# Scan of a hybrid backbone: copies out of PSUM on one engine, and two buffers for the queries

## Chip, cores and metric

The kernel runs on one core of a Trainium2 chip. The metric is the time of one execution on the device in microseconds (us). Engines are named as in the profile: PE is TensorE, PEld its weight loads, DVE is VectorE, ACT is ScalarE, POOL is GpSimd, SP is SyncE, which issues most of the DMAs.

## The reference

Two layers of a backbone over 512 latent tokens and 256 context tokens, 1024 wide: the first mixes tokens by attention, the second by a state that is updated token by token (RWKV-7), once in each direction. Each mixer is followed by a SwiGLU block. The change lies in the second mixer, whose core is

```python
def _wkv_scan(S0, decay, k, v, kk, a, r, reverse):
    ...
    def step(S, inp):
        w_t, k_t, v_t, kk_t, a_t = inp[:5]
        sa = jnp.einsum('bhvk,bhk->bhv', S, -kk_t)
        S = (S * w_t[:, :, None, :] + sa[..., None] * (kk_t * a_t)[:, :, None, :]
             + v_t[..., None] * k_t[:, :, None, :])
        y = jnp.einsum('bhvk,bhk->bhv', S, inp[5]) if len(inp) == 6 else None
        return S, y
    S, ys = lax.scan(step, S0, tuple(jnp.moveaxis(z, 1, 0) for z in xs), reverse=reverse)
```

for 16 heads of 64 channels. The context's tokens have no queries `r` and give no `y`; their last state starts the scan of the latents. After it come a group norm, a gate, an output projection and the second SwiGLU block.

## The kernel before

The scan is done in blocks of 64 tokens: inside a block by matrix products, from block to block by a state of 64 x 64 per head. The tokens are cut into three parts p of 256 tokens: p = 0 is the context, p = 1 and 2 are the latents, taken from the front for direction d = 0 and from the back for d = 1. The 16 heads are two groups g of 8 heads, each held in four tiles f. A stage is a pair (p, g); there are six (line 1351).

Three functions make up a stage:

- `elem(p, f)` (lines 1063 to 1142) makes a tile's elementwise quantities: decays, keys, and for p > 0 the queries. It loads `kt` (keys) and `rt` (queries) from DRAM with `load` (line 1034 for p > 0, a DMA issued by SyncE). VectorE makes `R`, the decayed queries (line 1107), and overwrites `rt` with the product with the keys (line 1109); TensorE reads that once more for the bonus `bp` (line 1114), and only then is `rt` free. For p = 0 nothing is loaded into `rt`; it is scratch memory there (lines 1098 and 1099). `rt` has one buffer (`bufs=1`). `elem` also sends matrices out for the scan (lines 1096, 1097, 1104, 1108) and fills `AB`, the triangular blocks that are to be inverted.
- `invert(st)` (lines 1145 to 1203) inverts the blocks of one group by substitution, as a long row of short VectorE instructions (lines 1158, 1163, 1167, 1169) between block transposes (1149, 1172, 1173), and then merges 32 x 32 blocks by small matmuls (1184, 1198, 1200) into `Xs`.
- `scan(p, g)` (lines 1235 to 1317) goes through four steps i. A step decays the state to `S` (line 1251), copies it into `Tt` (1252, 1253), transposes a block of keys (1262, 1263), for p > 0 forms `GR` (1273, 1274), and then runs this chain:

```python
pp = ...                                              # 1281: 32 matmuls
nc.scalar.copy(Pb[HS[0], :, :, 0], pp[HS[0]])         # 1282
nc.vector.tensor_copy(Pb[HS[1], :, :, 1], pp[HS[1]])  # 1283
pu = ...                                              # 1287: 16 matmuls, with Xs
nc.scalar.copy(Tt[HS[0], 0], pu[HS[0]])               # 1289
nc.vector.tensor_copy(Tt[HS[0], 1], pu[HS[1]])        # 1290
pn = ...                                              # 1296: 32 matmuls, then Sn = pn + S (1301)
```

`HS[0]` and `HS[1]` are the lower and the upper 64 partitions. `pp` and `pu` are PSUM tiles of 128 x 512 fp32, each copied out in two halves of 64 x 512: one by ScalarE, one by VectorE. `Sn` is the next step's state. For p > 0 the step's output `py` (lines 1310, 1311) is copied (1316) and sent to DRAM.

Lines 1351 to 1360 set the program's order: scan of a stage, inversion of the next, `elem` of the one after. It is not the order on the engines. The kernel is built with a scheduler that simulates a timeline (line 1494) and places the instructions of `scan`, `invert`, `elem` and, at the end, `readout` between one another on each engine; an engine then runs its own queue in order. A tile pool adds waits where a buffer is used again. Before the first stage with queries, `project_r` (line 1320) computes the queries into DRAM; the pool `sB` (line 1344) is laid over the memory that it used. The tile `R` and the step's `GR`, `Rb` and `y` lie in `sB`. Behind the scan, `readout` (line 1386) loads the outputs of both directions and applies norm and gate; then come the output projection and the SwiGLU block.

Of the kernel before, what the change touches and what calls it, by code (L numbers as in the profile page):

```python
# [10 lines left out]
F32 = mybir.dt.float32  # L11
# [6 lines left out]
P = 128  # L18
# [15 lines left out]
HS = (slice(0, 64), slice(64, 128))  # L34
# [3 lines left out]
def tile_hybrid_backbone(ctx: ExitStack, tc: tile.TileContext, a: dict, out: bass.AP, dbg=None, stop=None, start=None):  # L38
    nc = tc.nc
# [462 lines left out]
    def pool(stack, name, bufs=1, side="left", psum=False):  # L502
        kw = {"space": PSUM} if psum else {"side": side}
        return stack.enter_context(tc.tile_pool(name=name, bufs=bufs, reuse_waits="tile", **kw))
# [305 lines left out]
    with ExitStack() as rw:  # L810
# [200 lines left out]
        slot_pool = {}  # L1011
# [4 lines left out]
        tm = pool(tms, "tm")  # L1016
# [15 lines left out]
        def load(t, src, p, f):  # L1032
            if p:
                nc.sync.dma_start(out=t, in_=src[:, f, 2 - p:4 - p])
                return t
            nc.sync.dma_start(out=t[:, 0], in_=src[:, f, 3])
            return t[:, 0:1].to_broadcast([P, 2, 256])
# [25 lines left out]
        def elem(p, f):  # L1063
            lat = p > 0
# [3 lines left out]
            if n + 1 < len(tiles):  # L1068
                front(*tiles[n + 1])
            kt = load(tm.tile([P, 2, 256], F32, name="kt", tag="kt"), d_k, p, f)  # L1070
            rt = tm.tile([P, 2, 256], F32, name="rt", tag="rt", bufs=1)
            if lat:
                load(rt, d_r, p, f)
            AR = ARs[n % 2]
# [131 lines left out]
        with ExitStack() as vv:  # L1206
            pv = pool(vv, "pv", 3, psum=True)
            for f in range(4):
                elem(0, f)
            invert(0)  # L1210
            wp = pool(vs, "wpj", side="right")
            vt_ = pool(vv, "vt", 2)
            for b in range(4):
                wh, wl = load_split(wp, wp, a["rwkv_wrkv"][0, 2, :, 256 * b:256 * b + 256], KT, 256, "wd", piece=2)
                for i in (4, 5, 0, 1, 2, 3):
                    ps = pv.tile([P, 512], F32, name="pv", tag="pv")[:, 0:256]
                    tk = slice(P * i, P * i + P)
                    for k in range(KT):
                        nc.tensor.matmul(ps, vxh(k, tk), wh[:, k, :], start=(k == 0), stop=False)
                        nc.tensor.matmul(ps, vxh(k, tk), wl[:, k, :], start=False, stop=False)  # L1220
                        nc.tensor.matmul(ps, vxl(k, tk), wh[:, k, :], start=False, stop=(k == KT - 1))
                    t = vt_.tile([P, 256], F32, name="vt", tag="vt")
                    nc.scalar.copy(t, ps)
                    nc.sync.dma_start(out=d_v[tk, 256 * b:256 * b + 256], in_=t)
            for f in range(4, 8):
                elem(0, f)
# [5 lines left out]
        Pb = sA.tile([P, 2, 4, 2, HD], F32, name="Pb")  # L1232
        nc.gpsimd.memset(Pb, 0.0)

        def scan(p, g):
# [3 lines left out]
            for i in range(4):  # L1239
                pos = (i, 3 - i)  # L1240
                first = p == 0 and i == 0
                Tt = sA.tile([P, 2, 4, 2, HD], F32, name="T", tag="T", bufs=2)
# [34 lines left out]
                pp = pC.tile([P, 2, 4, HD], F32, name="pp", tag="pq", bufs=2)  # L1277
# [2 lines left out]
                        for h in range(2):  # L1280
                            nc.tensor.matmul(pp[HS[h], d, f, :], fs[f][kr, h, d, pos[d], :], Tt[kr, d, f, h, :], start=True, stop=True)
                nc.scalar.copy(Pb[HS[0], :, :, 0], pp[HS[0]])
                nc.vector.tensor_copy(Pb[HS[1], :, :, 1], pp[HS[1]])
                pu = pC.tile([P, 4, 2, HD], F32, name="pu", tag="pq", bufs=2)
                for f in range(4):
                    for d in range(2):
                        nc.tensor.matmul(pu[HS[d], f].rearrange("p h e -> p (h e)"), Xs[:, f, d, pos[d], :],
                                         Pb[:, d, f].rearrange("p h e -> p (h e)"), start=True, stop=True)
                nc.scalar.copy(Tt[HS[0], 0], pu[HS[0]])
                nc.vector.tensor_copy(Tt[HS[0], 1], pu[HS[1]])  # L1290
                if (p, i) != (2, 3):
                    pn = pC.tile([P, 2, 4, HD], F32, name="pn", tag="pq", bufs=2)
                    for d in range(2):
# [58 lines left out]
        for s, (p, g) in enumerate(stages[:-1]):  # L1352
            scan(p, g)
            invert(s + 1)
            if s + 2 < len(stages):
                p2, g2_ = stages[s + 2]
                for f in range(4 * g2_, 4 * g2_ + 4):
                    elem(p2, f)
        tms.close()
        scan(2, 1)  # L1360
        sc_s.close()
    if stop == "scan":
# [135 lines left out]
```

## Time and profile before

| | |
|---|---|
| runs before | 2259.92, 2272.34 and 3232.45 us, median 2272.34 |
| profiled execution | 2262.3 us |
| its span | 2260.6 us, granted clock 0.933 |
| first step of the scan, first `pp` matmul (line 1281) | 1310.5 us after the span's start |
| steps of the scan as a row (from the first `Sn`) | about 1388 to 1796 us |
| `R` (line 1107), 16 instructions | 1406.9 to 1664.9 us |
| loads of `rt`, 16 | issue to landing 3.1 / 3.6 / 4.9 us (least, median, most) |
| TensorE, VectorE, ScalarE busy, whole span | 89%, 74%, 49% |

The span goes from the first to the last instruction of the core. A row of a group reads: line, engine, operation, output<-input, shapes, count, then busy time and mean duration in ns, then the idle time of the engine just before these instructions and what ended it. A row in order of time begins with start and duration in us and ends with the idle time ahead of it and its releaser, in brackets. A row of waits says who waited for whom, the total in us, how often, and the longest. Matmuls overlap, so their durations don't add up to PE's time.

### The profile page before, as it was taken

What the parts mean: (1) busy time and instruction counts of PE and PEld (TensorE: products, weight loads), DVE (VectorE), ACT (ScalarE), POOL (GpSimd) and SP (SyncE); (2) the same over time, 40 slices, a digit from 0 to 9 for tenths busy, and PEclk for the clock granted to TensorE, in tenths of its full rate; (3) what the DMA queues carried; (4) which work ended last, traced back from release to release, by engine and by line L of the source; (5) the groups of instructions that cost most, each with busy time, mean ns of one, the idle gap of its engine ahead of it and who ended that gap; (6) DMA issues with size and microseconds to landing.
All of it is one profiled execution on the core that took longest, in us unless ns stands there. A gap on an engine that the chain in (4) does not pass through costs nothing. (4 is left out here: it accounts for less than half of the span.)

```text
span 2260.6 us, 43038 instructions
## 1 busy us (share of the span) xinstructions
PE 2006.4 (89%) x16566; PEld 1773.0 (78%) x16566; DVE 1668.6 (74%) x3167; ACT 1111.3 (49%) x2274; POOL 688.3 (30%) x564
## 2 busy tenths in 40 slices
PE   6999999898999999995998978766878686999998
PEld 4995555697999999994867957655767586899998
DVE  4565555669777677769475599888696778899996
ACT  5446556655333333336243764855553465444443
POOL 1110000126344444413132231220110325666661
PEclk7999999998999999997988989986988988999999
DMA  8206762353222122212335674873644654332332
GB/s 304 69 21 219 236 228 87 137 162 113 83 66 75 56 85 66 67 47 66 103 116 186 178 220 135 230 200 95 195 137 134 195 173 130 123 103 85 112 96 74
DMA packets 250078, 294.13 MB, mean 130 GB/s; under 512 B 36201, under 2 KB 176721, under 8 KB 249489
## 3 DMA queue, kind: packets, MB, share of 16 engines
q1 hardware_dynamic: 249152, 290.52, 41.3%
q8 instruction: 131, 2.15, 0.4%
q10 hardware_dynamic: 352, 0.60, 0.1%
q14 instruction: 75, 0.61, 0.1%
q0 software_dynamic: 368, 0.26, 0.1%
HBM read 228.40 MB, written 50.33 MB: 123 GB/s over the span
## 5 line engine op out<-in xcount | busy, mean ns | idle before, releaser
L445 PE MATMUL yps<-gh,wu 128*128 128x384 f32 (+2 forms) x1120 | 324.3, 345 | 0.0
L258 DVE SCALAR_TENSOR_TENSOR xT<-yps,modT,xT 128x384 f32<-128x384 f32 (+3 forms) x360 | 185.3, 537 | 126.5 <-PE yps L445 107.7
L239 ACT CAST wu<-wr 128x512 fp32r<-128x512 f32 x276 | 168.6, 619 | 167.8 <-PE A L395 56.8
L239 ACT CAST wu<-ws 128x512 fp32r<-128x512 f32 x176 | 109.1, 621 | 220.5 <-PE yps L445 60.8
L445 PEld LDWEIGHTS yps<-gh,wu 128*128 128x128 f32 x1120 | 202.5, 189 | 11.4
L241 POOL TENSOR_TENSOR wu<-wr,wu 128x512 fp32r<-128x512 f32 x86 | 128.5, 1494 | 241.1 <-ACT wu L239 212.6
L445 PE MATMUL yps<-gl,wu 128*128 128x384 f32 (+2 forms) x560 | 192.9, 345 | 0.0
L349 POOL TENSOR_TENSOR ws<-wr 128x512 f32<-128x512 f32 x88 | 130.1, 1484 | 145.6 <-DMA wr<-in_ffn_wg_dram 79.4
L241 DVE TENSOR_TENSOR wu<-wr,wu 128x512 fp32r<-128x512 f32 x190 | 162.7, 861 | 13.5 <-ACT wu L239 13.0
L241 DVE TENSOR_TENSOR wu<-ws,wu 128x512 fp32r<-128x512 f32 x111 | 136.9, 1234 | 17.6 <-ACT wu L239 17.3
L241 POOL TENSOR_TENSOR wu<-ws,wu 128x512 fp32r<-128x512 f32 x65 | 99.3, 1528 | 66.5 <-ACT wu L239 65.8
L228 PE MATMUL yps<-oTh,wu 128*128 128x384 f32 (+1 forms) x512 | 110.5, 308 | 1.1 <-ACT wu L239 1.0
L445 PEld LDWEIGHTS yps<-gl,wu 128*128 128x128 f32 x560 | 105.8, 189 | 4.3
L731 DVE TENSOR_REDUCE mx<-S 128x1 f32<-128x768 f32 (+1 forms) x96 | 74.7, 778 | 45.7 <-PE S L728 45.0
L395 PE MATMUL C<-x5h,wu 128*128 128x384 f32 (+1 forms) x352 | 87.6, 326 | 14.0 <-ACT x5h L312 12.2
L1136 POOL TENSOR_SCALAR_AFFINE_SELECT GA<-GA 64x512 f32<-64x512 f32 x48 | 43.1, 898 | 185.0 <-ACT GA L1134 183.7
L743 ACT COPY PT<-PTp 128x384 f32<-128x384 f32 (+1 forms) x160 | 69.4, 466 | 53.8 <-PE PTp L742 53.6
L742 PEld LDWEIGHTS PTp<-ident,pr 128*128 128x128 f32 x448 | 50.2, 144 | 50.4 <-issue 24.4
L395 PE MATMUL A<-x1h,wu 128*128 128x384 f32 (+1 forms) x352 | 83.5, 313 | 4.7 <-POOL wu L241 2.3
L395 PE MATMUL B<-x2h,wu 128*128 128x384 f32 (+1 forms) x352 | 84.7, 309 | 2.2 <-POOL wu L241 2.1
L228 PEld LDWEIGHTS yps<-oTh,wu 128*128 128x128 f32 x512 | 85.0, 188 | 1.9 <-ACT wu L239 1.4
L241 POOL TENSOR_TENSOR wu<-mw,wu 128x512 fp32r<-128x512 f32 x2 | 2.9, 1458 | 265.3 <-ACT wu L239 265.3
(408 smaller groups left out, 6324.7 us busy)
## 6 DMA issues: line engine op xcount, KB each, us to landing
mw<-in_mod_w_dram SPq DMA_DIRECT2D x48, 1024.0 KB, 5.3
wr<-in_ffn_wg_dram SPq DMA_DIRECT2D x44, 512.0 KB, 4.2
wr<-in_ffn_wu_dram SPq DMA_DIRECT2D x44, 512.0 KB, 3.8
wr<-in_ffn_wd_dram SPq DMA_DIRECT2D x44, 512.0 KB, 3.9
d_b<-BK SPq DMA_DIRECT2D x24, 512.0 KB, 4.0
Bs<-d_b SPq DMA_DIRECT2D x48, 256.0 KB, 3.7
wraw<-in_rwkv_wrkv_dram SPq DMA_DIRECT2D x32, 256.0 KB, 3.2
wr<-in_rwkv_wo_dram SPq DMA_DIRECT2D x16, 512.0 KB, 4.5
```

Of the source, the lines that this page charges most:

```text
L228: nc.tensor.matmul(ps, w(k), x(k, sl), start=(k == 0 and i == 0), stop=(k == nk - 1 and i == 2))
L239: nc.scalar.copy(hi, raw)
L241: (nc.gpsimd if lane["n"] % 3 == 0 else nc.vector).tensor_tensor(out=lo, in0=raw, in1=hi, op=ALU.subtract)
L258: nc.vector.scalar_tensor_tensor(out=xT[:, f, t0:t1], in0=ps[:, t0 - sl.start:t1 - sl.start], scalar=modT[:, l, 8 * m + f, s:s + 1], in1=x ...
L349: nc.gpsimd.tensor_tensor(out=t, in0=x, in1=y, op=op)
L395: nc.tensor.matmul(ps, w[:, k], x[:, k], start=(k + j == 0), stop=(k == 3 and j == 2))
L445: nc.tensor.matmul(ps, u[k // 2][w][:, k % 2, fs], gs[k // 2][x][:, k % 2, sl], start=(k + j == 0), stop=(k == nk - 1 and j == 2))
L731: nc.vector.tensor_reduce(out=mx, in_=S[:, :nk * P], axis=AX.X, op=ALU.max)
L742: nc.tensor.transpose(ps[:, t - t0, :], pr_[:, P * t:P * t + P], ident)
L743: nc.scalar.copy(PT[h][:, t0:t1, P * qt:P * qt + P], ps[:, :t1 - t0, :])
L1136: nc.gpsimd.affine_select(out=ga, in_=ga, compare_op=ALU.is_gt, fill=0.0, base=0, pattern=[[0, 2], [0, 4], [sg, 64]], channel_multiplier=-sg)
```

## The change

It has two parts. In `elem`, `rt` of the stages with queries comes from the pool `sB` and has two buffers; the context's tiles keep the one buffer in `tm`. In `scan`, the second half of both copies out of PSUM (lines 1283 and 1290) goes from VectorE to ScalarE. Nothing that is computed changes, and no line is added.

```diff
@@ elem
             kt = load(tm.tile([P, 2, 256], F32, name="kt", tag="kt"), d_k, p, f)
-            rt = tm.tile([P, 2, 256], F32, name="rt", tag="rt", bufs=1)
+            rt = (slot_pool["B"] if lat else tm).tile([P, 2, 256], F32, name="rt", tag="rt", bufs=2 if lat else 1)
             if lat:
                 load(rt, d_r, p, f)
@@ scan
                 nc.scalar.copy(Pb[HS[0], :, :, 0], pp[HS[0]])
-                nc.vector.tensor_copy(Pb[HS[1], :, :, 1], pp[HS[1]])
+                nc.scalar.copy(Pb[HS[1], :, :, 1], pp[HS[1]])
...
                 nc.scalar.copy(Tt[HS[0], 0], pu[HS[0]])
-                nc.vector.tensor_copy(Tt[HS[0], 1], pu[HS[1]])
+                nc.scalar.copy(Tt[HS[0], 1], pu[HS[1]])
```

Since the scheduler places the instructions anew, the queues of the engines differ around these lines too, from the first inversions on; the prediction shows the places that it speaks of.

## The prediction

> **What bounds the kernel now.** I read the page's first part, then the busy time of each engine by stretch, because a share of the whole span mixes stages with different limits. The page says that TensorE is the busiest engine:
>
> ```profile
> span 2260.6 us, 43038 instructions
> PE 2006.4 (89%) x16566; PEld 1773.0 (78%) x16566; DVE 1668.6 (74%) x3167; ACT 1111.3 (49%) x2274; POOL 688.3 (30%) x564
> ```
>
> In the scan it is another. These are busy times by stretch (columns: stretch, its length, then PE, weight loads, VectorE, ScalarE and GpSimd, granted clock, DMA share, GB/s):
>
> ```profile
> 1380.00:1500.00 120.00, 96.51 (x1350) 78.76 (x1348) 103.56 (x210) 81.17 (x178) 26.57 (x33) 0.91 0.68 193
> 1500.00:1550.00 50.00, 26.78 (x372) 20.62 (x372) 45.39 (x110) 20.12 (x42) 8.89 (x11) 0.70 0.47 133
> 1550.00:1650.00 100.00, 85.11 (x1610) 76.75 (x1612) 72.93 (x145) 62.24 (x133) 15.04 (x20) 0.91 0.57 165
> 1650.00:1713.00 63.00, 45.85 (x888) 40.61 (x884) 59.26 (x138) 28.64 (x60) 5.65 (x8) 0.79 0.40 115
> 1713.00:1796.00 83.00, 67.71 (x1291) 60.71 (x1290) 49.12 (x89) 39.72 (x77) 18.69 (x17) 0.93 0.56 174
> ```
>
> VectorE is busy 86% of the first stretch, 91% of the second and 94% of the fourth; it runs the inversions and the elementwise work for the next group, with the scan's copies between them. In the third stretch TensorE leads (85%), in the fifth too (82%), and there the steps of the scan wait for one another. The 24 steps with their neighbours fill 416 us. Before and after them the change adds and removes nothing, so the difference is made here.
>
> **The copies.** All copies of the two kinds, busy time and mean ns, then the idle time of the engine ahead of them and who ended it:
>
> ```profile
> L1283 DVE COPY Pb<-pp 64x512 f32<-64x512 f32 x24 | 16.7, 695 | 6.9 <-ACT Pb L1282 6.4
> L1290 DVE COPY T<-pu 64x512 f32<-64x512 f32 x24 | 16.5, 688 | 12.4 <-ACT T L1289 12.2
> L1289 ACT COPY T<-pu 64x512 f32<-64x512 f32 x24 | 13.9, 579 | 28.5 <-PE pu L1287 27.5 <-ACT z L1427 0.5 <-ACT W L1186 0.3
> L1282 ACT COPY Pb<-pp 64x512 f32<-64x512 f32 x24 | 13.9, 578 | 19.7 <-PE pp L1281 19.6
> ```
>
> The change takes 48 copies from VectorE, 16.7 + 16.5 = 33.2 us, and gives ScalarE 48 of the same size, 48 x 0.579 = 27.8 us. The two halves of a pair already run one after the other: VectorE sat idle 6.4 and 12.2 us until ScalarE's half was done. One pair where VectorE was free, one where it was not, and one that held back the step, in order of time:
>
> ```profile
> 1569.10 0.58 ACT L1282 COPY Pb<-pp 64x512 f32<-64x512 f32 x1 [1.45 <-PE pp L1281]
> 1569.71 0.69 DVE L1283 COPY Pb<-pp 64x512 f32<-64x512 f32 x1 [1.01 <-ACT Pb L1282]
> 1704.90 0.58 ACT L1282 COPY Pb<-pp 64x512 f32<-64x512 f32 x1 [2.06 <-PE pp L1281]
> 1710.39 0.69 DVE L1283 COPY Pb<-pp 64x512 f32<-64x512 f32 x1
> 1711.14 1.97 PE L1287 MATMUL pu<-Pb,Xs 128*64 128x128 f32 x16 [0.80 <-DVE Pb L1283]
> ```
>
> In the first pair VectorE starts 0.03 us after ScalarE's end, so the pair costs 1.30 us, and on one engine 2 x 0.58 = 1.16. In the second VectorE stands in its own queue behind the inversion, the copy starts 4.9 us late, and the matmuls of `pu` wait for it. On ScalarE the halves stand next to each other in all 24 steps:
>
> From scan(2, 0) on, ScalarE before (`Xs_13736` is the inverse for the next stage, `Bt` the transposed blocks, `y` the step's output):
>
> ```order
> L1289 COPY T<-pu 64x512
> L1263 COPY Bt<-BTp 128x512 x2
> L1252 COPY T<-S 64x8x64
> L1316 COPY y<-py 128x512
> L1282 COPY Pb<-pp 64x8x64
> L1289 COPY T<-pu 64x512
> L1191 COPY Xs_13736<-O_18032 32x4x4x32 x2
> ```
>
> and the same place now:
>
> ```order
> L1289 COPY T<-pu 64x512
> L1290 COPY T<-pu 64x512
> L1263 COPY Bt<-BTp 128x512 x2
> L1252 COPY T<-S 64x8x64
> L1316 COPY y<-py 128x512
> L1282 COPY Pb<-pp 64x8x64
> L1283 COPY Pb<-pp 64x8x64
> L1289 COPY T<-pu 64x512
> L1290 COPY T<-pu 64x512
> ```
>
> Each second half now follows its first with nothing between; what queues behind it (`Bt`, and the inverse's pieces) starts 0.58 us later.
>
> A page speaks against the move. The Trainium skill, ScalarE: Activation LUTs, Rules for kernel authors, says to give simple operations to VectorE, since it can be up to about three times as fast per element in bf16. By that rule the copies would get dearer; the rows disagree for these fp32 copies out of PSUM, 579 ns on ScalarE against 695 and 688.
>
> **The loads of rt.** VectorE's waits for them by stretch, and one of them in order of time:
>
> ```profile
> DVE R L1107 <- DMA rt<-d_r: 7.2, 5, 2.1
> ...
> DVE R L1107 <- DMA rt<-d_r: 2.5, 1, 2.5
> ...
> DVE R L1107 <- DMA rt<-d_r: 11.0, 3, 6.3
> ...
> DVE R L1107 <- DMA rt<-d_r: 1.2, 2, 0.8
> ```
>
> ```profile
> 1596.11 1.93 SPq L1256 DMA_DIRECT2D Bs<-d_b  x2
> 1598.14 0.38 SPq L1034 DMA_DIRECT2D rt<-d_r  x1
> ```
>
> ```profile
> 1601.93 0.69 DVE L1107 TENSOR_TENSOR R<-rt,eU 128x512 f32<-128x512 f32 x1 [6.27 <-DMA rt<-d_r]
> 1603.83 0.69 DVE L1290 COPY T<-pu 64x512 f32<-64x512 f32 x1
> 1604.58 0.78 PE L1296 MATMUL pn<-T,Bt 128*64 128x64 f32 x16 [4.29 <-DVE T L1290]
> ```
>
> In all 21.9 us of 11 waits. The longest is told by the rows: with one buffer the load is issued late, behind a step's loads of `Bs`, it lands after 3.8 us, VectorE stands for 6.27, the copy at its back is late, and TensorE waits 4.29 for that. In SyncE's queue the load of the third tile of group (2, 0) stood here, before:
>
> ```order
> L1269 DMA Rb0_13738<-d_q2_11680 64x256 x2
> L1245 DMA T_15690<-d_v_10403 64x512
> L1317 DMA d_y_10404<-y_15562 128x512
> L1245 DMA T_15690<-d_v_10403 64x512
> L1269 DMA Rb0_13738<-d_q2_11680 64x256 x2
> L1256 DMA Bs_15822<-d_b2_11674 128x512 x2
> L1034 DMA rt_16355<-d_r_10401 128x512
> L1108 DMA d_q4_11682<-R_16374 256x4x64
> ```
>
> and stands here now:
>
> ```order
> L1034 DMA kt_16266<-d_k_10399 128x512
> L1034 DMA rt_16268<-d_r_10401 128x512
> L1047 DMA wa0_11689<-in_rwkv_w2_dram 64x128
> L1034 DMA rt_16355<-d_r_10401 128x512
> L1096 DMA AR1_11688<-lw_16162 64x512
> L1097 DMA GA_16275<-lw_16162 64x512
> ```
>
> It went ahead of a whole tile's loads; it still waits for a buffer, but for the one of two tiles back. I count the 21.9 us as nearly gone. The first such load must now wait until the projection of the queries gives up the memory under the new buffers: between 0 and one landing, 3.8 us, once; the tile `R` lies there already and must wait as well, so I take 0.
>
> **The sum, stretch by stretch.** VectorE's moved copies in the five stretches, first `Pb`, then `T`:
>
> ```profile
> 1380.00:1500.00 120.00, 4.41 (x7) 0.91 0.68 193
> 1500.00:1550.00 50.00, 1.15 (x2) 0.70 0.47 133
> 1550.00:1650.00 100.00, 4.17 (x6) 0.91 0.57 165
> 1650.00:1713.00 63.00, 2.08 (x3) 0.79 0.40 115
> 1713.00:1796.00 83.00, 4.17 (x6) 0.93 0.56 174
> ```
>
> ```profile
> 1380.00:1500.00 120.00, 4.84 (x7) 0.91 0.68 193
> 1500.00:1550.00 50.00, 0.69 (x1) 0.70 0.47 133
> 1550.00:1650.00 100.00, 4.12 (x6) 0.91 0.57 165
> 1650.00:1713.00 63.00, 2.05 (x3) 0.79 0.40 115
> 1713.00:1796.00 83.00, 4.69 (x7) 0.93 0.56 174
> ```
>
> First stretch: 4.41 + 4.84 = 9.2 of copies and 7.2 of waits for `rt`, 16.4 us at most. VectorE keeps 94 us of work, but TensorE has 96.5 and ScalarE goes from 81.2 to 89.3, three engines close together. I take a little over half, 9.
>
> Second and fourth: 1.84 + 4.13 = 6.0 of copies and 2.5 + 1.2 = 3.7 of waits, 9.7 us. VectorE stays alone at the top (TensorE 72.6 and ScalarE 48.8 of 113), so I take it all, 9.5.
>
> Third: 8.3 of copies and 11.0 of waits, 19.3, and pairs that get shorter; but TensorE is busy 85.1 of 100, which leaves at most 14.9. I take 11.
>
> Fifth: VectorE is not the limit, so its freed 8.9 us count only through the steps' latency. Between ScalarE's end and VectorE's start lie 11.5 us over 13 pairs, the first at 1713.20 and the last at 1793.22, 4.31 of them in one (ScalarE's half at 1775.61, VectorE's at 1780.50, below), and 13 x (0.69 - 0.58) = 1.4 come from the quicker copy: 12.9 at most. Part of it lies under the matmuls of `py` and the readouts, so I take half, 6.
>
> ```profile
> 1775.61 0.58 ACT L1282 COPY Pb<-pp 64x512 f32<-64x512 f32 x1 [3.09 <-PE pp L1281]
> 1780.50 0.69 DVE L1283 COPY Pb<-pp 64x512 f32<-64x512 f32 x1
> ```
>
> Together 9 + 9.5 + 11 + 6 = 35.5 us, with 16.4 + 9.7 + 14.9 + 12.9 = 54 as the ceiling. The added 27.8 us of ScalarE cost nothing as long as its idle time covers them: it is idle 416 - 231.9 = 184 us here. Without that cover all 27.8 would show. What is late next is TensorE, with 322 us of 416.
>
> The profiled execution took 2262.3 us, 1.7 around its span; of the three runs shown (2259.92, 2272.34, 3232.45) it lies between the lower two, whose mean is 2266.1. From that, 2266.1 - 35.5 = **2231**; from the profiled execution itself it would be 2227.
>
> **The rivals.** (1) All of it comes: the ceiling, 2266.1 - 54 = 2212. For it speaks that a quicker step also releases the next; against it that three engines lie close in the first stretch.
>
> (2) ScalarE takes over. It runs in order, its second halves now stand ahead of `tanh`, `exp` and the copies that feed the inversions, and in the first stretch it reaches 89 of 120. Then only the second and fourth stretch gain: 2266.1 - 9.5 = 2257. Against it: VectorE hardly waits for ScalarE today but in the pairs.
>
> (3) The pair ran side by side on two engines and now runs in a row, so that each step loses 1.16 - 0.69 = 0.47 us: 24 x 2 x 0.47 = 22.6, 2289. The rows speak against it (VectorE starts 0.03 us after ScalarE's end). The rule behind it: the Trainium skill, PSUM — Partial Sum Buffer, says that ScalarE and VectorE can read PSUM at the same time at full bandwidth, as long as they don't meet in one bank; this trace shows no pair that did.
>
> (4) Slower: SyncE's queue. The loads of `rt` now stand further forward, and one that finds no free buffer holds what is behind it, the loads of `AR` and `GA`, on which the next matrices and the inversion hang. At a landing each, 16 x 3.8 = 61 us and nothing gained in return: 2327. It decides once the wait for the buffer exceeds the slack of the loads behind it. Against it: the buffer is the one of two tiles back.
>
> **How the numbers follow.** Chances: the forecast 0.54, all of it 0.20, ScalarE 0.16, side by side 0.02, SyncE 0.08. A measurement of this kernel can tell about 2%, 45 us, from no change: below 2227. Rival 1 lies there, and about a quarter of the forecast's own spread (2215 to 2245), 0.14: faster 0.34. The rest of the forecast with rivals 2 and 3 is the same, 0.58; rival 4 is slower, 0.08. The range goes from 2203, a little under the ceiling, to 2262, a little over rival 2.
>
> **What would show it.** Right: ScalarE's copy groups at lines 1282, 1283, 1289 and 1290 with 24 each near 580 ns; VectorE's 33 us gone; waits of `R` for `rt` under 6 us; the matmuls of `pu` and `pn` held by ScalarE alone; the scan's 416 us near 380. Wrong: VectorE's idle time grows by as much as its work shrinks, with ScalarE as releaser (rival 2); SyncE's waits at lines 1034, 1096 and 1097 grow (rival 4); or the work behind the scan, 465 us long, gets longer by what the scan gains.

## The result and the profile after

The changed kernel takes 2247.2 us (median of 6 runs, 2243.89 to 2252.62); the kernel before took 2264.56 in the same comparison (median of 6; one of them, of 3232.45 us, is a slow execution that the ratio leaves out). The ratio is 0.993, with a 95% interval of 0.9909 to 0.9951: 0.7% faster, some 16 us. The forecast was 2231, a gain of 35.5. The direction came out, the size is less than half. The two profiled executions had nearly the same granted clock, 0.933 before and 0.934 after, so the 15.6 us between their spans are not the clock's.

The page's first part and VectorE's waits in the scan (from 1300 to 1800 us; who waited for whom: us in total, times, longest), changed kernel:

```profile
span 2245.0 us, 43057 instructions
...
PE 2005.4 (89%) x16566; PEld 1769.6 (79%) x16566; DVE 1638.5 (73%) x3119; ACT 1138.0 (51%) x2322; POOL 684.3 (30%) x564
```

```profile
DVE Sn L1301 <- PE pn L1296: 16.1, 5, 7.4
DVE GR L1274 <- PE A L1273: 12.5, 7, 9.0
DVE R L1107 <- DMA rt<-d_r: 11.7, 9, 2.8
...
DVE E L1149 <- ACT AB L1141: 7.0, 3, 5.9
```

Before, two of these were

```profile
DVE GR L1274 <- PE A L1273: 3.0, 5, 2.1
...
DVE Sn L1301 <- PE pn L1296: 2.4, 2, 1.6
```

and there was no wait for `AB`. VectorE has 30.1 us less work, ScalarE 26.7 more. The span is 15.6 us shorter, so about half of VectorE's freed time came back as idle time, and these rows say where. The waits for `rt` fell from 21.9 to 11.7, not to nearly nothing. One sign that the prediction named came out: `pn` and `pu` no longer wait for VectorE. TensorE had waited 11.2 us at `pn` and 4.8 at `pu` for VectorE's halves, and 6.7 at `pn` for ScalarE's; now it waits 4.1 and 1.9, for ScalarE's copies.

The groups of the copies:

```profile
L1290 ACT COPY T<-pu 64x512 f32<-64x512 f32 x24 | 14.0, 583 | 0.6
L1283 ACT COPY Pb<-pp 64x512 f32<-64x512 f32 x24 | 14.0, 582 | 0.5
L1289 ACT COPY T<-pu 64x512 f32<-64x512 f32 x24 | 13.9, 577 | 17.9 <-PE pu L1287 12.3 <-issue 5.4
L1282 ACT COPY Pb<-pp 64x512 f32<-64x512 f32 x24 | 13.8, 576 | 22.0 <-PE pp L1281 21.9
```

All 24 second halves stand behind their first: 0.5 and 0.6 us of idle time ahead of 24 copies. Adding up the time from the start of a pair's first half to the end of its second, over the rows in order of time, gives 59.5 us for `Pb` and 54.6 for `T` before, 28.2 and 28.4 now. The steps' pairs are 57 us shorter, and the scan only 16.

Busy time by stretch (columns as in the prediction), cut at places in the program near those of before:

```profile
1376.40:1490.50 114.10, 92.08 (x1295) 74.42 (x1293) 86.65 (x177) 83.00 (x178) 22.26 (x31) 0.91 0.66 187
1490.50:1541.60 51.10, 30.43 (x364) 22.84 (x364) 48.06 (x114) 26.47 (x56) 8.99 (x13) 0.71 0.66 182
1541.60:1641.60 100.00, 84.04 (x1657) 75.68 (x1658) 73.24 (x152) 68.94 (x144) 12.16 (x19) 0.91 0.60 171
1641.60:1697.30 55.70, 42.83 (x886) 38.40 (x884) 44.41 (x104) 32.72 (x68) 5.96 (x8) 0.87 0.37 111
1697.30:1780.30 83.00, 68.15 (x1294) 61.03 (x1294) 47.26 (x97) 45.03 (x85) 19.45 (x17) 0.89 0.57 170
```

The third is as long as before, with nearly the same work of TensorE (84.04 us, 85.11 before). Cutting at the starts of four copies, from the rows in order of time, says the same more sharply:

| place | before | after | gained since the row above | forecast for it |
|---|---|---|---|---|
| first `Pb` of scan(1, 0) | 1509.2 | 1499.7 | 9.5 | 9 |
| last `Pb` of scan(1, 1) | 1661.9 | 1653.5 | -1.1 | about 15 (second stretch 4.3, third 11) |
| first `Pb` of scan(2, 1) | 1744.8 | 1728.7 | 7.7 | 5.3 and a part of the fifth's 6 |
| last `T` of the scan, its end | 1796.1 | 1780.3 | -0.3 | the rest of the 6 |

The work behind the scan took as long as before. In these two traces the first row and the second inversion gave what was forecast, though 3.6 of the 9.5 us had come by the first `Sn` (1387.9 before, 1384.3 after), at the very start of the forecast's first stretch. The middle, from scan(1, 0) to scan(1, 1), gave nothing. That the split is no property of the change alone is seen further down, where other orders of the instructions split the gain otherwise. One step of the middle in order of time, changed kernel:

```profile
1593.17 1.15 PE L1281 MATMUL pp<-T,GA 128*64 128x64 f32 x32
1594.37 0.58 ACT L1282 COPY Pb<-pp 64x512 f32<-64x512 f32 x1 [1.81 <-PE pp L1281]
1594.97 0.58 ACT L1283 COPY Pb<-pp 64x512 f32<-64x512 f32 x1
1595.20 1.04 PE L1262 MATMUL BTp<-ident,Bs 128*128 128x128 f32 x8
...
1596.51 0.59 PE L1053 MATMUL z<-ta,wa 128*128 128x256 f32 x2
1596.65 0.57 ACT L1134 COPY GA<-A 64x512 f32<-64x512 f32 x1
1597.04 1.09 PE L1287 MATMUL pu<-Pb,Xs 128*64 128x128 f32 x16
1597.25 0.36 ACT L1140 COPY AB<-A 32x256 f32<-32x256 f32 x1
...
1598.27 0.26 ACT L1141 COPY AB<-A 32x128 f32<-32x128 f32 x1
1598.54 0.58 ACT L1289 COPY T<-pu 64x512 f32<-64x512 f32 x1
1599.15 0.58 ACT L1290 COPY T<-pu 64x512 f32<-64x512 f32 x1
...
1600.06 1.03 PE L1296 MATMUL pn<-T,Bt 128*64 128x64 f32 x28
1601.24 0.69 DVE L1301 TENSOR_TENSOR Sn<-pn,S 128x512 f32<-128x512 f32 x1 [7.45 <-PE pn L1296]
```

The pair of `Pb` ends at 1595.55, but TensorE is at other work until 1597.04. The pair of `T` stands in ScalarE's queue behind `GA` and the pieces of `AB`. VectorE's queue has come to `Sn` and stands 7.45 us for the step. In this step VectorE is not the limit: TensorE and ScalarE are, each in the order of its own queue.

### The profile page after: what moved, and what is told of

Same layout as the page of the kernel before. It is cut to its first block, busy times and chain, and to the rows that moved or that the text cites. A ratio compares the mean times of both kernels' runs of the same rounds, so it can differ in the third digit from the quotient of the medians.

```text
span 2245.0 us, 43057 instructions
## 1 busy us (share of the span) xinstructions
PE 2005.4 (89%) x16566; PEld 1769.6 (79%) x16566; DVE 1638.5 (73%) x3119; ACT 1138.0 (51%) x2322; POOL 684.3 (30%) x564
## 4 chain that ended last, share of the span: by engine, by line
PE 63%; DVE 15%; DMA 8%; issue 5%; ACT 4%; POOL 3%; SPq 1%; DVEq 0%; POOLq 0%; ACTq 0%
PE yps L445 13%; PE A L395 8%; PE B L395 5%; PE C L395 5%; PE yps L228 5%; PE po L747 3%; PE S L728 2%; PE PTp L742 2%; PE mps L126 2%; PE pj L228 2%; PE qps L595 2%; DVE wu L241 2%; PE qps L597 2%; PE qps L596 2%; PE pr L1337 2%
## 5 line engine op out<-in xcount | busy, mean ns | idle before, releaser
L241 POOL TENSOR_TENSOR wu<-wr,wu 128x512 fp32r<-128x512 f32 x86 | 123.3, 1434 | 236.1 <-ACT wu L239 212.4
L1136 POOL TENSOR_SCALAR_AFFINE_SELECT GA<-GA 64x512 f32<-64x512 f32 x48 | 37.6, 783 | 199.4 <-ACT GA L1134 196.4
L395 PE MATMUL C<-x5h,wu 128*128 128x384 f32 (+1 forms) x352 | 85.2, 319 | 14.4 <-ACT x5h L312 12.3
L395 PE MATMUL A<-x6h,wu 128*128 128x384 f32 (+1 forms) x352 | 80.4, 310 | 4.1 <-ACT x6h L312 3.5
```

The costliest lines, as they stand in the source:

```text
L241: (nc.gpsimd if lane["n"] % 3 == 0 else nc.vector).tensor_tensor(out=lo, in0=raw, in1=hi, op=ALU.subtract)
L395: nc.tensor.matmul(ps, w[:, k], x[:, k], start=(k + j == 0), stop=(k == 3 and j == 2))
```

## The experiments

Ratios are to the kernel before, run on the same chip, with a 95% interval; differences in us are differences of ratios times 2264. A trace is one execution, up to 8 us away from its kernel's median. Two theories stood at first: the gain is VectorE's 33 us of work ("load"), or the handing of half a pair from ScalarE to VectorE ("handoff").

**The copies alone** (`rt` with one buffer).

```diff
-            rt = (slot_pool["B"] if lat else tm).tile(..., bufs=2 if lat else 1)
+            rt = tm.tile(..., bufs=1)
```

> The second halves of both copies on ScalarE, the queries' load with its one buffer as before. Load theory (the gain is VectorE's 33 us, part of which came back as new waits): this part alone gives most of the 17 us, 11 to 16 us below the kernel before, and VectorE's waits of R for rt stay at 20 us or more. Rival, the loads: the 10 us by which those waits fell are the larger share, and this part gives 5 to 8 us. Rival, the order (the scheduler's new order alone moves the time by as much): anything within 10 us either way, with the difference not at the copies.

2248.71 us, ratio 0.993 [0.9902, 0.9958]: the whole gain, while VectorE's waits for `rt` stay nearly what they were (21.9 before):

```profile
DVE R L1107 <- DMA rt<-d_r: 20.6, 9, 5.8
```

**The buffers alone** (both second halves back on VectorE).

```diff
-                nc.scalar.copy(Pb[HS[1], :, :, 1], pp[HS[1]])
+                nc.vector.tensor_copy(Pb[HS[1], :, :, 1], pp[HS[1]])
...
-                nc.scalar.copy(Tt[HS[0], 1], pu[HS[1]])
+                nc.vector.tensor_copy(Tt[HS[0], 1], pu[HS[1]])
```

> Two buffers for the queries' load, the copies as before. Load theory: 0 to 5 us below the kernel before, since VectorE keeps its work. Loads theory: 8 to 12 us below, with the waits of R for rt near 10 us. Order theory: anything within 10 us either way.

2259.76 us, ratio 0.9991 [0.997, 1.0011]: nothing that can be measured. VectorE's waits in the scan:

```profile
DVE Sn L1301 <- PE pn L1296: 12.5, 6, 6.6
DVE T L1290 <- ACT T L1289: 12.3, 8, 2.6
DVE R L1107 <- DMA rt<-d_r: 9.8, 6, 2.8
```

The waits for `rt` fell by 12.1 us, and those for `pn` rose by 10.1: VectorE stood at another place of its queue. Nor did the loads of `rt` hold up SyncE's queue: it stands 23.7 us at line 1096, as before (23.9), and the time is not longer.

**Both halves on VectorE**, with two buffers.

```diff
-                nc.scalar.copy(Pb[HS[0], :, :, 0], pp[HS[0]])
-                nc.scalar.copy(Pb[HS[1], :, :, 1], pp[HS[1]])
+                nc.vector.tensor_copy(Pb[HS[0], :, :, 0], pp[HS[0]])
+                nc.vector.tensor_copy(Pb[HS[1], :, :, 1], pp[HS[1]])
...
-                nc.scalar.copy(Tt[HS[0], 0], pu[HS[0]])
-                nc.scalar.copy(Tt[HS[0], 1], pu[HS[1]])
+                nc.vector.tensor_copy(Tt[HS[0], 0], pu[HS[0]])
+                nc.vector.tensor_copy(Tt[HS[0], 1], pu[HS[1]])
```

> Two buffers for the queries' load, and both halves of both copies on VectorE: no handoff inside a pair, 48 copies of 0.69 us more on VectorE than before. Load theory: slower than the kernel with the two buffers alone by 13 to 20 us, so 10 to 18 us above the kernel before. Handoff theory (the gain is the wait between the two engines in each pair): faster than the two buffers alone by 5 to 13 us.

2273.93 us, ratio 1.004 [1.0021, 1.006]; against the buffers alone 0.0049, 11 us slower. Here too no half is handed over, and the pairs are nearly as short as on ScalarE (33.8 and 33.6 us over all steps, in place of 28). The handoff theory wanted 5 to 13 us less time than with the buffers alone; it came out 11 us more, further away than a new order of instructions was worth below (7 us). So the handing over is not what the gain was. What counts is in whose queue the work lies. That can mean two things, which this run doesn't tell apart: VectorE's amount of work, or that a step's copies stand in VectorE's queue behind the inversion.

**A new order alone**: the kernel before, with a step's loads of `Bs` written ahead of its loads of `T`.

```diff
+                Bs = sA.tile([P, 2, 4, P], F32, name="Bs", tag="Bs", bufs=2)
+                for d in range(2):
+                    nc.sync.dma_start(out=Bs[:, d], in_=d_b[st][pos[d], :, d])
                 for d in range(2):
                     t0 = T0(p, d) + 64 * pos[d]
                     nc.sync.dma_start(out=Tt[HS[1], d], in_=d_v[t0:t0 + 64, 512 * g:512 * g + 512])
...
-                Bs = sA.tile([P, 2, 4, P], F32, name="Bs", tag="Bs", bufs=2)
-                for d in range(2):
-                    nc.sync.dma_start(out=Bs[:, d], in_=d_b[st][pos[d], :, d])
```

> The kernel before with the same work, only the two loads of Bs of a step written ahead of its two loads of T: what a new order from the scheduler is worth by itself. Order theory: 5 us or more away from the kernel before, either way. Load theory: within 3 us.

2270.18 us, ratio 1.0032 [1.0013, 1.0051]. The scheduler places everything anew after any edit, and that alone was worth 7 us here. Differences below that are not read as causes in what follows, and the main kernels were run with the same move too (there the tile of `T` is still taken ahead of that of `Bs`). It is called the second order below; each kernel has queues of its own in it, so two orders are two samples, and not a fixed order held against another.

**The loads of rt**: a third buffer, and the loads issued by GpSimd.

```diff
-            rt = (slot_pool["B"] if lat else tm).tile(..., bufs=2 if lat else 1)
+            rt = (slot_pool["B"] if lat else tm).tile(..., bufs=3 if lat else 1)
```

```diff
-                load(rt, d_r, p, f)
+                nc.gpsimd.dma_start(out=rt, in_=d_r[:, f, 2 - p:4 - p])
```

> The changed kernel with a third buffer for rt. In the changed kernel VectorE still waits 11.7 us for loads of rt (21.9 before), and SyncE's queue stands 51.9 us at the loads of Rb until py is done. If a buffer is what is still short: waits for rt under 4 us, time 2240 to 2244. If the loads are late because they stand behind the loads of Rb in SyncE's queue: waits for rt stay above 8 us, time within 4 us of the changed kernel's 2247 but for the scatter of a new order of instructions, some 5 us.

> The changed kernel with the loads of rt issued by GpSimd instead of SyncE, still two buffers. If SyncE's queue is what makes them late: waits for rt under 4 us. If those waits are on the path, the time falls by most of them, to 2238 to 2242; if VectorE only waits somewhere else instead (for TensorE's pn and A, 28.6 us in the changed kernel), the time stays within 5 us of 2247.

2248.33 us, ratio 0.994 [0.9917, 0.9964], and 2246.09 us, 0.9927 [0.9898, 0.9956]: the changed kernel's time. VectorE's waits, third buffer, then GpSimd's loads:

```profile
DVE Sn L1301 <- PE pn L1296: 19.7, 5, 10.6
...
DVE R L1107 <- DMA rt<-d_r: 4.6, 2, 2.4
```

```profile
DVE Sn L1301 <- PE pn L1296: 23.7, 11, 5.4
...
DVE R L1107 <- DMA rt<-d_r: 4.4, 4, 2.8
```

Both edits take most of the waits that were left (11.7 to 4.6 and 4.4), so neither the buffer nor SyncE's queue was the one cause, and both pay nothing: the wait for `pn` grows from 16.1 to 19.7 and 23.7. In the second order the changed kernel, with two buffers, waits 19.2 us for `rt`, and is no slower for it (2242.41 us, below). The loads of `rt` are not on the path.

**One part of the copies at a time**, and each in the second order.

```diff
-                nc.scalar.copy(Pb[HS[1], :, :, 1], pp[HS[1]])
+                nc.vector.tensor_copy(Pb[HS[1], :, :, 1], pp[HS[1]])
```

```diff
-                nc.scalar.copy(Tt[HS[0], 1], pu[HS[1]])
+                nc.vector.tensor_copy(Tt[HS[0], 1], pu[HS[1]])
```

> The changed kernel with the second half of Pb back on VectorE, so that only the copies of T are on one engine: 24 copies moved instead of 48. If the gain goes with VectorE's work, half of it is left: 2254 to 2258. If the handing from ScalarE to VectorE counted, which cost 12.2 us of waits at T and 6.4 at Pb, about two thirds are left: 2251 to 2254. If T alone carries it, 2247.

> The changed kernel with the second half of T back on VectorE: only the copies of Pb are on one engine. With only T on one engine the time was 2262.85, no gain (ratio 1.0003). If the copies of Pb carry the whole gain: 2247. If the two parts gain only together, since either of them alone leaves a copy of each step in VectorE's queue behind the inversion: 2259 to 2264. If each 16 us of VectorE's work are worth about 8 us and the run with T alone fell on a bad order of instructions: 2252 to 2258.

> The changed kernel with one thing moved: a step's loads of Bs are written ahead of its loads of T. Nothing is done otherwise; the scheduler places all instructions anew. It sizes what a new order alone is worth on the changed kernel; the same move cost the kernel before 0.3% (2270.2). If the order is worth 5 us or more either way: outside 2243 to 2251. If not: within it.

> The kernel with only the copies of T on one engine (2262.85, no gain), with the loads of Bs written ahead of those of T. If that kernel's missing gain was bad luck with the order: 2250 to 2258, since another order brings the half gain back. If T alone is worth nothing: 2260 or more.

> The kernel with only the copies of Pb on one engine, in the other order of writing (loads of Bs ahead of loads of T). In that order the kernel before took 2270.2, T alone 2270.9 and both parts 2242.4. If Pb alone carries the gain there: 2242 to 2248. If the two parts gain only together: 2262 to 2272. If each is worth half and T alone was unlucky twice: 2254 to 2260.

| second halves on ScalarE | first order: us, ratio | second order: us, ratio |
|---|---|---|
| none (one buffer) | 2264.56, 1 | 2270.18, 1.0032 [1.0013, 1.0051] |
| none (two buffers) | 2259.76, 0.9991 [0.997, 1.0011] | not run |
| `T` | 2262.85, 1.0003 [0.9986, 1.0019] | 2270.93, 1.0045 [1.0026, 1.0064] |
| `Pb` | 2258.33, 0.9981 [0.9964, 0.9997] | 2255.44, 0.9965 [0.9949, 0.9981] |
| both (the change) | 2247.2, 0.993 [0.9909, 0.9951] | 2242.41, 0.9918 [0.9886, 0.9951] |

The rows below the first have two buffers. In the second order the change is worth 0.0114, some 26 us, where it was 16 in the first: its size is known no better than that. `T` alone is worth nothing in either order, though it takes 16.5 us from VectorE; on top of `Pb` it is worth 0.5% in both. VectorE's waits with `T` alone, first order:

```profile
DVE Sn L1301 <- PE pn L1296: 20.0, 8, 4.0
...
DVE Pb L1283 <- ACT Pb L1282: 8.1, 6, 2.3
```

Of `T` alone one thing is seen, against the buffers alone: the 12.3 us that VectorE had waited at `T` are gone, and the wait at `Sn`, the next thing that it does for the same step, has grown from 12.5 to 20.0; the pairs of `Pb`, 60.0 us over all steps, are as long as in the kernel before. For `Pb` alone the traces say more than the times. By the end of the scan it had gained 12.0 us (1784.1 against 1796.1) and in the second order 15.8 (1785.4 against 1801.2), most of what both parts gain there (15.8 and 25.5); behind the scan its two traces are 4 to 5 us longer than those of the kernel before (468.6 and 468.4 us, against 464.4 and 463.7). Why the parts gain more together than singly was not settled. That `T` alone is worth nothing speaks against a plain theory of VectorE's amount of work.

**The price of work on each engine**: the changed kernel with copies of a scratch tile `scr` onto itself, which nobody reads, written into each step.

```diff
+                if "scr" in slot_pool:
+                    for _ in range(3):
+                        nc.vector.tensor_copy(slot_pool["scr"], slot_pool["scr"])
...
+        scr = sB.tile([P, 512], F32, name="scr")
+        nc.gpsimd.memset(scr, 0.0)
+        slot_pool["scr"] = scr
```

```diff
+                if "scr" in slot_pool:
+                    for _ in range(2):
+                        nc.scalar.copy(slot_pool["scr"], slot_pool["scr"])
...
```

> The changed kernel with three extra copies of 128x512 on VectorE in each step from the first query stage on (16 steps, 48 copies, 0.46 us each by the row of line 1253: about 22 us), of a scratch tile onto itself, which nobody reads. It gives VectorE work of the size that the change took away, but outside the steps' chain. If VectorE's amount of work sets the time at the price seen (0.4 to 0.5 us for each us): 2256 to 2259. If what the change gave was the shorter way from pp to Sn alone: 2247, within 4.

> The changed kernel with two extra copies of 128x512 on ScalarE in each of the same 16 steps (32 copies of about 0.6 us, 19 us), of a scratch tile onto itself. It prices ScalarE's work, which the prediction took at nothing. If ScalarE has cover: 2247, within 4. If ScalarE's work now costs as VectorE's did: 2255 or more.

> The changed kernel with the extra copies on VectorE, in the other order of writing (loads of Bs ahead of those of T). In the first order these were 72 copies in all 24 steps, 33.0 us, and not 48 as was expected then; they cost 23 us (2270.56 against 2247.2), 0.7 us for each. If that price is the work's: 2242.4 + 23 = 2265 in this order, within 6. If it was the order's: 2242 to 2252.

> The changed kernel with the extra copies on ScalarE, in the other order of writing. In the first order these were 48 copies, 29.7 us, and cost 11 us (2258.14 against 2247.2), 0.37 us for each. If that price is the work's: 2242.4 + 11 = 2253 in this order, within 6. If ScalarE's work has cover and the 11 us were the order's: 2238 to 2247.

The two groups, first order (count, least, median and most in ns, first and last start in us):

```profile
L1278 DVE COPY scr<-scr x72: 381/420/906, 1406.1 to 1516.1; 128x512 f32<-128x512 f32 x72
```

```profile
L1278 ACT COPY scr<-scr x48: 601/618/649, 1412.7 to 1529.5; 128x512 f32<-128x512 f32 x48
```

The copies are written into all 24 steps and not 16, as the first two expectations had it, which makes them nearly the change's own amounts: 33.0 us on VectorE and 29.7 on ScalarE, for 33.2 and 27.8. But they did not run step by step. No other instruction reads `scr`, and the scheduler placed them all in one stretch, in the second order too (1410 to 1532 and 1407 to 1534 us). There both engines are well filled already: from 1406.1 to 1516.5 us VectorE is busy 84.70 and ScalarE 84.40 of 110.40 us in the changed kernel. Of the copies that the change moved, only 9.2 of 33 us lay in the stretch from 1380 to 1500.

The times: with VectorE's copies 2270.56 us (ratio 1.0038 [1.0024, 1.0052]) and 2269.17 (1.0031 [1.0014, 1.0048]); with ScalarE's 2258.14 (0.9976 [0.9962, 0.9989]) and 2258.26 (0.9976 [0.996, 0.9993]). Against the changed kernel in the same order, 33 us of VectorE cost 24.5 and 25.6 us, about 0.76 for each us; 29.7 us of ScalarE cost 10.4 and 13.1, about 0.40. The intervals leave some 6 to 8 us on each difference, so both prices are above zero, and no finer than that. They are prices of this stretch. In the runs with VectorE's copies the pairs are as short as in the changed kernel (28.2 and 28.5 us in the first order), and still its gain is gone: VectorE's work counts here by itself, without standing between the parts of a step.

As prices of the whole scan they don't hold. They would give 33.2 x 0.76 - 27.8 x 0.40 = 14 us for the change, near the 16 measured in the first order, but about 7 for `T` alone, which was worth nothing. What the change's work is worth on either engine at its own places was not measured singly.

**More work off VectorE**: the second half of `S` into `T` on ScalarE too, in both orders, and then the inverse's lower blocks as well.

```diff
-                    nc.vector.tensor_copy(Tt[HS[0], :, :, 1], S[HS[1]])
+                    nc.scalar.copy(Tt[HS[0], :, :, 1], S[HS[1]])
```

```diff
-                    nc.vector.tensor_copy(Xs[lo(h), :, d, :, 0:32], o[lo(h), :, d])
+                    nc.scalar.copy(Xs[lo(h), :, d, :, 0:32], o[lo(h), :, d])
```

> The changed kernel with the second half of the copy of S into T (line 1253, 22 copies of 0.46 us on VectorE, 10.1 us in all) on ScalarE too, about 13.5 us there. If the time still follows VectorE's work at the price seen so far (17 us of time for 33 us of work), it falls by 5 us, to 2242. If ScalarE has become the dearer engine or the copy's half in a row (0.6 us a step) counts: 2249 to 2260.

> The fastest kernel so far (the change, and the second half of S into T on ScalarE, 2237.2), in the other order of writing. If its 10 us over the changed kernel were work and not order: below the changed kernel in that order, 2242.4, by 5 to 10 us: 2232 to 2237. If they were order: 2242 or more.

> The changed kernel with the second half of S into T (line 1253) and the lower blocks of the inverse (line 1190, 24 copies, 10.8 us on VectorE) on ScalarE as well: 20.9 us of VectorE's work moved beyond the change, about 28 us on ScalarE. The first of the two alone gave 2237.2 (10 us less than the changed kernel for 10.1 us of work). If VectorE's work still sets the time: 2226 to 2234. If ScalarE is now the dearer engine, which the wait of the inversion for ScalarE's AB (14.3 us with the first alone, none before) speaks for: 2237 or more.

The first took 2237.23 us, ratio 0.9885 [0.9857, 0.9912], and 2234.55 in the second order, 0.9875 [0.9855, 0.9895]: faster than the changed kernel by 0.0045 and 0.0043, 10 us in both, and the intervals leave some 8 us on each. This is the fastest version found. The prices of the stretch above would give 10.1 x 0.76 - 13.6 x 0.40 = 2 us; why it gives 10 was not tried further. With the inverse's blocks as well the gain over the changed kernel is gone again: 2246.31, 0.9927 [0.9907, 0.9946] (one order only). VectorE's wait for `AB`, with `S` alone and then with both:

```profile
DVE E L1149 <- ACT AB L1141: 14.3, 3, 8.7
```

```profile
DVE E L1149 <- ACT AB L1141: 11.7, 3, 9.5
```

In both the inversion starts late for `AB`, which ScalarE copies in the order of its queue; in the kernel before that wait was not there at all. But it is no longer in the slower of the two, so it doesn't explain what the inverse's blocks cost. That stays open; the trace with them is also 8 us faster than its kernel's median.

## Why the prediction was half right

**What held.** The gain came from the copies and went with VectorE's queue: the copies alone gave all of it (ratio 0.993), and heaping the other halves on VectorE made the kernel slower than before (1.004). That VectorE bounds the stretch of the first inversions, as the prediction read, is borne out by 33 us of other work on it there, which cost 25. The durations held too, 576 to 583 ns on ScalarE. Rival 3, that the pairs had run side by side, falls with the rows: in none of the 48 pairs of before do the halves overlap. Rival 4, that the loads of `rt` would hold up SyncE's queue, falls with the buffers alone at 0.9991.

**The loads of rt, "21.9 us nearly gone": the step that failed.** The waits only fell to 11.7, and taking them away gave no time: nothing with the buffers alone (0.9991), nothing lost with the copies alone, which keep 20.6 us of them, and nothing more where a third buffer or GpSimd's queue took most of the rest. They were idle time of an engine that then waited for `pn` instead. The sum had added them to the freed work as if both lay on the path; by their share of the waits and copies in the first four stretches, some 14 of its 35.5 us came from them. The rows that the prediction shows, where TensorE waits 4.29 us behind one such load, are right; one wait that holds back a step is not yet the sum of all eleven.

Without them 35.5 - 14 leaves some 21 us for the copies. Measured are 16 in the first order and 26 in the second, so the rest of the sum fits within what an order is worth. (The 416 us hold 23 of the 24 steps; the first step's copies run at 1314 us, ahead of them.)

**The stretches: not to be judged from one order.** Gains up to the same four places, from the rows in order of time:

| place | change, first order | copies alone | change, second order | forecast |
|---|---|---|---|---|
| first `Pb` of scan(1, 0) | 9.5 | 2.5 | 15.2 | 9 |
| from there to the last `Pb` of scan(1, 1) | -1.1 | 5.4 | 11.3 | about 15 |
| to the first `Pb` of scan(2, 1) | 7.7 | 3.4 | 3.6 | 5.3 and a part of the 6 |
| to the end of the scan | -0.3 | 3.0 | -4.5 | the rest of the 6 |

The first two columns are against the kernel before, the third against the kernel before in the second order. The middle takes 152.7 us before, 153.8 with the change and 147.3 with the copies alone; in the second order 160.2 without and 148.9 with the change; and 137.0 with `S` on ScalarE too. So "nothing came" in the third stretch, as "9.5 for 9" in the first, is a reading of one order, and that the first fits its forecast is luck as far as these traces show. TensorE's matmuls are the same in all of these, so TensorE's work is no floor at 153; the step at 1593 us shows what lies in between, other work of TensorE and ScalarE between the parts of a step.

**"The added 27.8 us of ScalarE cost nothing": open.** ScalarE was idle 184 us of 416, and that was taken for cover. Two things speak against it: the step at 1593 us shows `T` standing behind `GA` and `AB`, and the inversion waits for `AB` (7.0 us, none before). Extra work on ScalarE cost 0.35 and 0.44 us for each us in two orders, but all of it in the stretch from 1407 to 1534 us, where ScalarE has little room and where the prediction had itself taken only a little over half. For `S`, 13.6 us more on ScalarE did no visible harm. So rival 2's mechanism is seen at places, and its price at the change's own places is not known.

**Fifth, 6 us for shorter pairs:** not seen, -0.3 and -4.5 us from scan(2, 1) on with the change, 3.0 with the copies alone. The pairs did get shorter, there as everywhere, but half of 57 us of pair latency was not half of a gain.

Whether the copies gained by taking work from VectorE or by taking a step's copies out of its queue behind the inversion is not separated. Extra work shows that VectorE's work counts by itself in one stretch; `T` alone, 16.5 us less work and no gain, shows that the amount is not all. Against the queue's place speaks that with the buffers alone TensorE already waited less for VectorE's halves (8.1 us at `pn` and `pu`, 16.0 before), and gained nothing.

## What to carry to other kernels

Idle time of the limiting engine that ends on a DMA is a gain only if nothing else ends just behind it: 12 us of such waits were taken away here and nothing was gained. Before it is counted, look what that engine would wait for next. Price a moved instruction at both ends and at the place where it runs: where VectorE and ScalarE were both three quarters busy, 33 us more on VectorE cost 25 us and 30 us more on ScalarE about 12. Look in the trace where an added probe really ran; the ones written into every step ran in under a third of the scan here. And where a scheduler places the queues anew after any edit, run an edit that changes the order alone: it was worth 7 us of 2264 here, it moved single stretches by more, and only what shows in two orders is the edit's.

## What the runs showed of the hardware

For these fp32 copies the engine that is faster goes with where the operand lies. Out of PSUM a 64x512 copy took 576 to 583 ns on ScalarE and 688 to 695 on VectorE; from SBUF to SBUF, with `S` into `T`, 617 on ScalarE and 461 on VectorE:

```profile
L1253 DVE COPY T<-S 64x512 f32<-64x512 f32 x22 | 10.1, 461 | 0.9
```

```profile
L1253 ACT COPY T<-S 64x512 f32<-64x512 f32 x22 | 13.6, 617 | 0.5
```

(changed kernel, then with `S` on ScalarE; on VectorE the mean of this copy was between 422 and 517 ns in the other runs). The Trainium skill, Perfetto Trace Analysis, Optimizing Scalar/DVE Operations, gives an overhead for each instruction of about 125 ns on VectorE against 51 on ScalarE for PSUM, and 60 against 93 for SBUF. The rows agree on which engine is ahead in each case. They time whole copies and not the overhead alone, so the sizes can't be held against each other.
